# Hybrid block on one core: a ninth up tile in seven half products, adding transfers moved ahead, and a changed step into the MLP

## The chip, the cores and the metric

The kernel runs on 1 core of one Trainium2 chip. The metric is the device time in microseconds; the time before is 696.63 us, the median of 3 runs (695.25 to 696.77).

## The reference, cut to what matters

One layer of a trunk with x of 512 tokens by 1024 features. Attention of three kinds (A: differential, B: forgetting, C: chunked) is concatenated and goes through one out-projection; then comes a gated MLP of 2 x 2816 columns with a causal convolution of width 3; then a gated embedding of p.

```
h = h + jnp.concatenate([o_a, o_b, o_c], axis=-1) @ w_out[i]
h = h + conv_gated_mlp(rms_norm(h, ln_ffn[i]), w_up[i], conv_w[i], conv_b[i], w_down[i])
gate = jax.nn.sigmoid(rms_norm(h, ln_ple[i]) @ w_ple_gate[i])
h = h + (p[i] @ w_ple_proj[i]) * gate
...
u = h @ w_up
for j in range(CONV_WIDTH):
    c = c + conv_w[j] * up[:, j:j + S]
gate, val = jnp.split(c, 2, axis=-1)
return (jax.nn.silu(gate) * val) @ w_down
```

## The kernel before, in words

Matrix products run in three terms: each operand is split into a high part (a cast by ACT, names ending in hi, h or ah) and a low part (a subtraction by DVE, names ending in lo, l or al), and mm3 (line 238) issues high x high, low x high and high x low. So each weight tile costs a load into w_raw on SP's queue, an ACT cast w_hi, a DVE split w_lo, and then matmuls.

After the attention come the out-projection (last_out, tiles wo), the squares of its result for the norm (sq, sums, pst), and the projection of p (ple_unit, tiles pp, copied by ACT to pps and stored). roots takes the mean square in pst through a logarithm and an exponential on ACT into rb; norm(k) makes hn, Th (ACT) and Tl (DVE), the right sides of the MLP.

The MLP has 22 tiles of 128 gate and 128 value columns. An up tile is done in one of two forms:
- plain (up_plain, line 1254): two products u of 8 x 3 matmuls of 512 tokens, 48 in all, in three pieces of 18, 18 and 12;
- seven half products (up_seven, line 1278): 7 products of 12 matmuls of 256 columns, in banks sX, sZ, sZ2 and sY, in six pieces. Their left sides use sums of weight blocks that are added beforehand in memory (usum); the results are combined in su by ACT copies and DVE additions. The first two products go to sX and sZ; then Z2, Y, X again (after the first addition of su), Y again, and X a third time (after the second addition of su, which needs Y's second product).

ACT and DVE then make the taps of the convolution (c<-u or c<-su, a first one on ACT and two, of 511 and 510 columns, on DVE for each half), the silu on ACT and the multiplication c<-c,c on DVE. The down projection (dn_X, dn_Y, dn_Z) takes four groups of tiles in products of 18 matmuls of 256 columns, also with sums of weights (dsum); for the last groups the right sides are the tiles xh and xl.

What sets the order: the string ORDER (line 49) lists the pieces of the MLP on PE: P a piece of a plain tile, S a piece of a tile in seven half products, D one down product; tiles_of reads from it which tiles have which form. Before, the first two tiles stand outside of it, and tiles 4, 6, 9, 10, 12, 14, 16 and 18 have seven half products. The tasks of ACT, DVE and POOL around them are ordered by a planner from costs and dependences and then kept in the order written. PE, ACT, DVE and POOL each execute their rows in that order.

The sums of weights need two things. copy_sum (line 835) copies a part of a prepared sum from the inputs to a work tensor (usum of 256 KB or dsum), on SP's queue, at most two in each slot of the attention; COPIES spreads them over the slots 20 to 45 by the number of sums. add_sums makes one adding transfer after the other on POOL's queue, four for a usum and eight for a dsum, two in flight at a time; two_adds issues the first of these by hand, at fixed places of the program.

Of the kernel before, what the change touches and what calls it, by code (L numbers as in the profile page):

```python
# [45 lines left out]
PHASES = (0, 6, 12, 18, 22)  # L46


ORDER = ("PPPPSSSSSPPSPPSSSSPSPPSPPDDDDDDDSPSSSSDSDDDPDDDSSSSSPSPPSSSSSPSPSSSDSSDDDSDPDDDDDDDDDPPPSSSSSPPSPSSSPSSPSPPPPPPP")


def tiles_of(order):

    f, n, tiles = 2, {"P": 0, "S": 0}, {"P": [], "S": []}
    for c in order:
        if c in n:
            if n[c] == 0:
                tiles[c].append(f)
                f += 1
            n[c] = (n[c] + 1) % {"P": 3, "S": 6}[c]  # L60
    assert f == NF and not any(n.values()), (f, n)
    return tiles["P"], tiles["S"]


PLAIN, SEVEN = tiles_of(ORDER)

# [11 lines left out]
def kernel(ctx: ExitStack, tc: tile.TileContext, x, xt0, xt, pt_in, small, bias_c,  # L78
# [33 lines left out]
    pe, act, dve, pool, sp = (Engine(e) for e in (nc.tensor, nc.scalar, nc.vector, nc.gpsimd, nc.sync))  # L112

    def bank(tag, name):
        return ps.tile([P, 512], F32, tag=tag, bufs={"z": 2, "s": 2, "t": 3, "o": 1}[tag], name=name)
# [122 lines left out]
    def mm3(acc, ah, al, bh, bl, first, last, **k):  # L238
        pe.matmul(acc, ah, bh, start=first, stop=False, **k)
        pe.matmul(acc, ah, bl, start=False, stop=False, **k)  # L240
        pe.matmul(acc, al, bh, start=False, stop=last, **k)
# [598 lines left out]
    def add_parts(key):  # L840

        v, _, more = sums_of(key)
        pairs = ((1, more[:, 0]), (2, more[:, 1]), (0, v[:, 1]), (3, v[:, 0]))
        if key[0] == "u":
            return [(v[:, i], q) for i, q in pairs]
        return [(v[:, i, j], q[:, j]) for i, q in pairs for j in range(2)]
# [59 lines left out]
    def last_out(j):  # L906
        for _ in out_unit(j, (6, 7), {k: wo[k, j // 4] for k in (6, 7)}, []):
            pass
# [8 lines left out]
    def mtmp(dt, m, name):  # L917
        return mp.tile([P, S * m], dt, tag="conv", bufs=CONV, name=name)
# [3 lines left out]
    def square(j):  # L922
        sq = mtmp(F32, 1, f"sq{j}")
        act.activation(sq, hj(j), AF.Square)
        return sq

    def total(tag, sums):

        pst = bank(tag, "pst")
        pe.matmul(pst, onec.broadcast_to([P, P]), sums, start=True, stop=True)  # L930
        return pst

    def roots(pst, rb, mt, sq):

        act.activation(rb, pst, AF.Ln, scale=1.0 / D, bias=epsc)
        dve.tensor_scalar(mt, pst, 1.0 / D, EPS, ALU.mult, ALU.add)
        act.activation(rb, rb, AF.Exp, scale=-0.5)
        dve.tensor_tensor(out=sq, in0=rb, in1=rb, op=ALU.mult)
        dve.scalar_tensor_tensor(sq, sq, -0.5, mt, ALU.mult, ALU.mult)
        dve.scalar_tensor_tensor(rb, sq, 1.5, rb, ALU.add, ALU.mult)  # L940
# [20 lines left out]
    def ple_product(j):  # L961
        PP[j] = acc = bank("tttzsttt"[j], f"pp_{j}")
        for k in range(2):
            a, b = (w[:, j % 4 * P : (j % 4 + 1) * P] for w in WPP[j // 4, k])
            mm3(acc, a, b, *pT[k], k == 0, k == 1)

    def ple_keep(j):
        pp = mtmp(F32, 1, f"pps_{j}")
        act.copy(pp, PP[j])
        sp.dma_start(out=pp_d[j], in_=pp)  # L970

    def ple_unit(j):
        ple_product(j)
        ple_keep(j)
# [210 lines left out]
    def add_sums():  # L1185

        state = {}

        def do(to, src):
            ins = pool.dma_start(out=to, in_=src, accum_op=ALU.add, max_dma_last_dim=6144).ins  # L1190
            state["all"] = [*state.get("all", ()), ins]
            if len(state["all"]) > 2:
                tc.add_manual_dep(ins, state["all"][-3].name, mybir.DependencyInfo(
                    mybir.DependencyClass.Sync, mybir.DependencyReason.DATA), reason="two adding transfers at a time")

        adds = EARLY_ADDS
        for _, *key in _sums:
            key = tuple(key)
            for to, src in add_parts(key):
                adds.append(Task("add", [("pool", 0.85), (f"acc{len(adds) % 2}", 4.8 if key[0] == "u" else 5.2)], lambda to=to, src=src: do(to, src),  # L1200
                                 adds[-1:] if key[0] == "u" and len(SUM_TASKS.get(key, ())) == 3 else adds[-2:-1]))
                SUM_TASKS.setdefault(key, []).append(adds[-1])
# [200 lines left out]
    def first_load():  # L1403
        q = loads.pop(0)
        q.do()
        q.end = 0.0

    def first_split(f, i, later=False):
        w = first_w[f][0][i]
        lows = [] if later else None  # L1410
        w.hi, w.lo = split(w.t, w.n, lows=lows)
        w.split.end = 0.0
        return lows[0] if later else None

    def two_adds():
        for q in [q for q in EARLY_ADDS if q.end is None][:2]:
            q.do()
            q.end = 0.0

    add_sums()  # L1420
    act.pinned = dve.pinned = pool.pinned = True
    sums, todo = None, ple_splits()
    loads = first_loads()
    for _ in range(2):
        first_load()
    todo += [lambda i=i: first_split(0, i) for i in range(2)]
    for j in range(KD):
        last_out(j)
        if 0 < j < KD - 1:
            todo[j - 1]()  # L1430
            if j > 2:
                first_load()
        elif j:
            todo[6]()
        sq = square(j)
        if j == 1:
            sums = mtmp(F32, 1, "sums")
            pool.tensor_tensor(out=sums, in0=last_sq, in1=sq, op=ALU.add)
        elif j > 1:
            (pool if j < KD - 2 else dve).tensor_tensor(out=sums, in0=sums, in1=sq, op=ALU.add)  # L1440
        last_sq = sq
    todo[7]()
    two_adds()
    for j in range(3):
        ple_unit(j)
    first_split(1, 0)
    ple_unit(3)
    rb2, work = (mp.tile([P, 7, H], F32, tag=tag, bufs=3, name=f"rb2_{tag}").rearrange("p j c -> p (j c)") for tag in ("ah", "al"))
    rb2 = rb2[:, :S]
    roots(total("o", sums), rb2, work[:, :S], work[:, S : 2 * S])  # L1450
    ple_unit(4)
    last_low = first_split(1, 1, True)
    norm(0)
# [106 lines left out]
    pieces = {"P": (f for f in PLAIN for _ in up_plain(f)), "S": (f for f in SEVEN for _ in up_seven(f)), "D": down_pieces()}  # L1560
    for c in ORDER:
        next(pieces[c])
# [263 lines left out]
```

## Time and profile before

| what | value |
|---|---|
| median of 3 runs | 696.63 us |
| the profiled execution | 695.37 us, span 693.6 us |
| mean granted TensorE clock | 0.998 |
| PE, DVE, ACT, POOL busy | 679.1, 560.6, 410.9, 236.0 us |
| DMA | 133.84 MB, mean 193 GB/s |
| first and last product of the MLP | 309.47 and about 644 us |

A row of the timeline gives the start, the duration, the engine, the line of the program, the operation with out<-in, the shape and, in brackets, how long the engine was idle ahead of it and what released it. A line of the chain gives start, length, engine and tile. Line 104 is the helper that issues almost every operation, so rows are told apart by tiles.

### The profile page before, as it was taken

What the parts mean: (1) busy time and instruction counts of PE and PEld (TensorE: products, weight loads), DVE (VectorE), ACT (ScalarE), POOL (GpSimd) and SP (SyncE); (2) the same over time, 40 slices, a digit from 0 to 9 for tenths busy, and PEclk for the clock granted to TensorE, in tenths of its full rate; (3) what the DMA queues carried; (4) which work ended last, traced back from release to release, by engine and by line L of the source; (5) the groups of instructions that cost most, each with busy time, mean ns of one, the idle gap of its engine ahead of it and who ended that gap; (6) DMA issues with size and microseconds to landing.
All of it is one profiled execution on the core that took longest, in us unless ns stands there. A gap on an engine that the chain in (4) does not pass through costs nothing.

```text
span 693.6 us, 12203 instructions
## 1 busy us (share of the span) xinstructions
PE 679.1 (98%) x4244; PEld 618.3 (89%) x4244; DVE 560.6 (81%) x1168; ACT 410.9 (59%) x799; POOL 236.0 (34%) x349
## 2 busy tenths in 40 slices
PE   8999999999999999999999999999999999999997
PEld 8988988988999988878899899989998898999886
DVE  6679887888878875689788987898888889888873
ACT  6656766767656754475476655456554566556821
POOL 5586675767575540231212111221112200000210
PEclk9999999999999999999999999999999999999999
DMA  9553579746745184279999799997999874462431
GB/s 307 216 168 98 155 241 265 232 165 162 287 136 178 44 266 138 91 184 242 175 269 244 133 266 241 274 232 176 248 278 277 181 197 140 141 234 99 156 122 60
DMA packets 57112, 133.84 MB, mean 193 GB/s; under 512 B 6454, under 2 KB 8118, under 8 KB 57052
## 3 DMA queue, kind: packets, MB, share of 16 engines
q1 hardware_dynamic: 45660, 107.60, 47.0%
q0 software_dynamic: 11104, 25.17, 22.2%
q8 instruction: 33, 0.54, 0.3%
q10 hardware_dynamic: 288, 0.30, 0.1%
q14 instruction: 27, 0.22, 0.1%
HBM read 125.83 MB, written 44.05 MB: 245 GB/s over the span
## 4 chain that ended last, share of the span: by engine, by line
PE 83%; DVE 8%; ACT 3%; POOL 3%; issue 2%; DMA 1%; SPq 0%; DVEq 0%; POOLq 0%; ACTq 0%
PE u L104 22%; PE dn_X L104 9%; PE pg L104 6%; PE C_z L104 5%; PE wo L104 5%; PE sX L104 5%; PE dn_Y L104 4%; PE B_z L104 4%; PE sY L104 3%; PE sZ L104 3%; PE A_z L104 3%; PE dn_Z L104 2%; PE A1b_z L104 1%; PE C_s L104 1%; PE B_s L104 1%
## 5 line engine op out<-in xcount | busy, mean ns | idle before, releaser
L104 DVE TENSOR_TENSOR w_lo<-w_raw,w_hi 128x768 fp32r<-128x768 f32 (+5 forms) x154 | 115.0, 786 | 9.5 <-ACT w_hi L104 9.3
L104 ACT CAST w_hi<-w_raw 128x768 fp32r<-128x768 f32 (+5 forms) x154 | 99.8, 687 | 35.9 <-PE sX L104 6.7
L104 PE MATMUL u<-Th,w_hi 128*128 128x512 f32 x224 | 87.0, 391 | 0.4 <-ACT Th L104 0.4
L104 PE MATMUL u<-Tl,w_hi 128*128 128x512 f32 x224 | 86.9, 390 | 0.0
L104 PE MATMUL u<-Th,w_lo 128*128 128x512 f32 x224 | 86.8, 390 | 0.0
L104 PEld LDWEIGHTS u<-Th,w_hi 128*128 128x128 f32 x224 | 42.0, 188 | 9.1 <-ACT Th L104 0.9
L104 PEld LDWEIGHTS u<-Th,w_lo 128*128 128x128 f32 x224 | 42.0, 188 | 9.0
L104 PEld LDWEIGHTS u<-Tl,w_hi 128*128 128x128 f32 x224 | 42.1, 188 | 8.1
L104 DVE SCALAR_TENSOR_TENSOR c<-u,cols,c 128x511 f32<-128x511 f32 (+1 forms) x56 | 41.0, 746 | 6.2 <-ACT c L104 5.7
L104 POOL DMA_DIRECT2D usum<-usum x16 | 13.0, 812 | 92.5 <-DMA usum<-in_w_up_dram 56.7
L104 PE MATMUL dn_X<-g_ah,w_hi 128*128 128x256 f32 x144 | 39.8, 276 | 0.0
L104 PE MATMUL dn_X<-g_ah,w_lo 128*128 128x256 f32 x144 | 39.8, 276 | 0.0
L104 PE MATMUL dn_X<-g_al,w_hi 128*128 128x256 f32 x144 | 39.8, 276 | 0.0
L104 PE MATMUL B_z<-B_h,Th 128*128 128x384 f32 x96 | 34.4, 358 | 0.8 <-DVE B_zn L104 0.6
L104 PE MATMUL C_z<-C_h,Th 128*128 128x384 f32 x96 | 34.3, 357 | 0.0
L104 POOL TENSOR_TENSOR sums<-sums,n_sq 128x512 f32<-128x512 f32 x3 | 3.9, 1291 | 86.9 <-ACT n_sq L104 86.8
L104 PE MATMUL B_z<-B_h,Tl 128*128 128x384 f32 x96 | 32.3, 337 | 0.0
L104 PE MATMUL C_z<-C_h,Tl 128*128 128x384 f32 x96 | 32.3, 337 | 0.0
L104 PE MATMUL C_z<-C_l,Th 128*128 128x384 f32 x96 | 32.2, 336 | 0.0
L104 PE MATMUL B_z<-B_l,Th 128*128 128x384 f32 x96 | 32.2, 335 | 0.0
L104 ACT ACTIVATE c<-u,cols 128x512 f32<-128x512 f32 x28 | 21.5, 775 | 16.0 <-PE u L104 14.6
L104 POOL DMA_DIRECT2D dsum<-dsum x16 | 13.0, 813 | 47.2 <-DMA dsum<-dsum 20.0
(504 smaller groups left out, 2384.0 us busy)
## 6 DMA issues: line engine op xcount, KB each, us to landing
w_raw<-in_w_up_dram SPq DMA_DIRECT2D x44, 384.0 KB, 6.1
dsum<-in_w_dsum_dram SPq DMA_DIRECT2D x12, 768.0 KB, 7.9
w_raw<-dsum SPq DMA_DIRECT2D x24, 384.0 KB, 5.0
usum<-in_w_usum_dram SPq DMA_DIRECT2D x32, 256.0 KB, 6.1
w_raw<-in_w_down_dram SPq DMA_DIRECT2D x18, 384.0 KB, 4.9
w_raw<-usum SPq DMA_DIRECT2D x16, 384.0 KB, 7.7
B_r<-in_w_in_dram SPq DMA_DIRECT2D x12, 384.0 KB, 3.6
C_r<-in_w_in_dram SPq DMA_DIRECT2D x12, 384.0 KB, 6.1
```

The costliest lines, as they stand in the source:

```text
L104: ins = getattr(self.eng, op)(*a, **k)
```

## The change

Three things:
1. ORDER has another order of pieces, with 11 plain tiles and 9 in seven half products: tile 15 is now one of these. With it go four more copies and four more adding transfers.
2. Two adding transfers are issued during the out-projection, as soon as POOL's last operation ahead of it is done; the two calls of two_adds that were there stay. So six transfers are issued ahead of the MLP by hand, four before.
3. In the step into the MLP first_split(1, 0), the split of the second tile's first weights (w_hi6 and w_lo6), comes one ple unit earlier, and the copy pps of unit 3 comes behind roots (logarithm and exponential).

```
-ORDER = ("PPPPSSSSSPPSPPSSSSPSPPSPPDDDDDDDSPSSSSDSDDDPDDDSSSSSPSPPSSSSSPSPSSSDSSDDDSDPDDDDDDDDDPPPSSSSSPPSPSSSPSSPSPPPPPPP")
+ORDER = ("PPPPSPSSSSPSPPSSSSPSPSPPPDDDDPDPDDSSDSSDSDDSDDDSSSSSPPSPSSSSSPSPSSSDPDSSDSDDDDDDDDDDDSSSSSSSSSSSPSPPSSSSSPSPPPPPPPP")
...
     add_sums()
+    last_sum_free = pool.last
     act.pinned = dve.pinned = pool.pinned = True
...
     todo += [lambda i=i: first_split(0, i) for i in range(2)]
+    with tc.issue_after(last_sum_free):
+        two_adds()
     for j in range(KD):
         last_out(j)
...
     two_adds()
-    for j in range(3):
+    for j in range(2):
         ple_unit(j)
     first_split(1, 0)
-    ple_unit(3)
+    ple_unit(2)
+    ple_product(3)
...
     roots(total("o", sums), rb2, work[:, :S], work[:, S : 2 * S])
+    ple_keep(3)
     ple_unit(4)
```

ple_unit(j) is ple_product(j), the matmuls, followed by ple_keep(j), the copy and the store.

**PE at tile 15.** In the changed kernel the rows of PE where the sixth product of tile 15 (sY15) ends and the seventh (sX15) begins:

```order
L104 MATMUL sY15_6367<-Th1_65,w_lo2_3991 128x256
L104 MATMUL sY15_6367<-Th1_65,w_hi2_3990 128x256
L104 MATMUL sY15_6367<-Tl1_67,w_hi2_3990 128x256
L104 MATMUL sY15_6367<-Th1_65,w_lo2_3991 128x256
L104 MATMUL sX15_6316<-xh_3881,w_hi1_3974 128x256
L104 MATMUL sX15_6316<-xl_3882,w_hi1_3974 128x256
L104 MATMUL sX15_6316<-xh_3881,w_lo1_3975 128x256
L104 MATMUL sX15_6316<-xh_3881,w_hi1_3974 128x256
```

In the kernel before, PE's rows behind the sixth product of tile 16, which has the same form in both:

```order
L104 MATMUL sY16_6436<-Th1_65,w_lo5_4022 128x256
L104 MATMUL sY16_6436<-Th1_65,w_hi5_4021 128x256
L104 MATMUL sY16_6436<-Tl1_67,w_hi5_4021 128x256
L104 MATMUL sY16_6436<-Th1_65,w_lo5_4022 128x256
L104 MATMUL u17_6503<-Th0_64,w_hi6_4057 128x512
L104 MATMUL u17_6503<-Tl0_66,w_hi6_4057 128x512
L104 MATMUL u17_6503<-Th0_64,w_lo6_4058 128x512
```

There pieces of a plain tile stand between the sixth product and the seventh; at the new tile 15 nothing does.

**ACT in the step into the MLP.** Before, from the last square on (pps the copies, w_hi6 the split that moves, rb2_ah the logarithm and the exponential):

```order
L104 CAST w_hi5_4021<-w_raw5_3902 128x768
L104 COPY pps_0_4034<-pp_0_4027 128x512
L104 COPY pps_1_4044<-pp_1_4037 128x512
L104 COPY pps_2_4054<-pp_2_4047 128x512
L104 CAST w_hi6_4057<-w_raw6_3953 128x768
L104 COPY pps_3_4068<-pp_3_4061 128x512
L104 ACTIVATE rb2_ah_4071<-pst_4073,epsc_76 128x512
L104 ACTIVATE rb2_ah_4071<-rb2_ah_4071 128x512
L104 COPY pps_4_4088<-pp_4_4081 128x512
```

The same rows in the changed kernel:

```order
L104 CAST w_hi5_4029<-w_raw5_3908 128x768
L104 COPY pps_0_4042<-pp_0_4035 128x512
L104 COPY pps_1_4052<-pp_1_4045 128x512
L104 CAST w_hi6_4055<-w_raw6_3961 128x768
L104 COPY pps_2_4066<-pp_2_4059 128x512
L104 ACTIVATE rb2_ah_4076<-pst_4078,epsc_76 128x512
L104 ACTIVATE rb2_ah_4076<-rb2_ah_4076 128x512
L104 COPY pps_3_4086<-pp_3_4069 128x512
L104 COPY pps_4_4096<-pp_4_4089 128x512
```

One copy has moved behind the two ACTIVATE rows, and the cast of w_hi6 ahead of one copy.

**DVE ahead of the last down products.** Before, from the first taps of tile 20 to those of tile 21 (c20 and c21 the gate halves, c42 and c43 the value halves):

```order
L104 SCALAR_TENSOR_TENSOR c20_7004<-u20_6820,cols_84,c20_7004 128x511
L104 SCALAR_TENSOR_TENSOR c42_7006<-u42_6839,cols_84,c42_7006 128x511
L104 SCALAR_TENSOR_TENSOR c20_7004<-u20_6820,cols_84,c20_7004 128x510
L104 SCALAR_TENSOR_TENSOR c42_7006<-u42_6839,cols_84,c42_7006 128x510
L104 TENSOR_TENSOR w_lo5_4022<-w_raw5_3902,w_hi5_4021 128x768
L104 TENSOR_TENSOR xl_3877<-sm_18_7001,xh_3876 128x1024
L104 TENSOR_TENSOR c20_7004<-c20_7004,c42_7006 128x512
L104 SCALAR_TENSOR_TENSOR c21_7061<-u21_6883,cols_84,c21_7061 128x511
L104 SCALAR_TENSOR_TENSOR c43_7064<-u43_6909,cols_84,c43_7064 128x511
L104 SCALAR_TENSOR_TENSOR c21_7061<-u21_6883,cols_84,c21_7061 128x510
L104 SCALAR_TENSOR_TENSOR c43_7064<-u43_6909,cols_84,c43_7064 128x510
L104 TENSOR_TENSOR c21_7061<-c21_7061,c43_7064 128x512
```

The same place in the changed kernel:

```order
L104 SCALAR_TENSOR_TENSOR c20_7065<-u20_6858,cols_84,c20_7065 128x511
L104 SCALAR_TENSOR_TENSOR c42_7067<-u42_6877,cols_84,c42_7067 128x511
L104 SCALAR_TENSOR_TENSOR c20_7065<-u20_6858,cols_84,c20_7065 128x510
L104 SCALAR_TENSOR_TENSOR c21_7095<-u21_6932,cols_84,c21_7095 128x511
L104 SCALAR_TENSOR_TENSOR c21_7095<-u21_6932,cols_84,c21_7095 128x510
L104 SCALAR_TENSOR_TENSOR c43_7099<-u43_6955,cols_84,c43_7099 128x511
L104 SCALAR_TENSOR_TENSOR c42_7067<-u42_6877,cols_84,c42_7067 128x510
L104 SCALAR_TENSOR_TENSOR c43_7099<-u43_6955,cols_84,c43_7099 128x510
L104 TENSOR_TENSOR w_lo0_3958<-w_raw0_3898,w_hi0_3957 128x768
L104 TENSOR_TENSOR xl_3882<-sm_18_7062,xh_3881 128x1024
L104 TENSOR_TENSOR c20_7065<-c20_7065,c42_7067 128x512
L104 TENSOR_TENSOR c21_7095<-c21_7095,c43_7099 128x512
```

The second tap of c42, a split of 768, the split of xl and the multiplication of c20 stood ahead of tile 21's taps and now stand behind the first of them. From there on to the split of dn3_0_1e, the first weights of the last group, the rows are the same in both kernels.

More of the change, by code (lines that the diff above doesn't have):

```diff
@@ L46 @@
 PHASES = (0, 6, 12, 18, 22)
-ORDER = ("PPPPSSSSSPPSPPSSSSPSPPSPPDDDDDDDSPSSSSDSDDDPDDDSSSSSPSPPSSSSSPSPSSSDSSDDDSDPDDDDDDDDDPPPSSSSSPPSPSSSPSSPSPPPPPPP")
+ORDER = ("PPPPSPSSSSPSPPSSSSPSPSPPPDDDDPDPDDSSDSSDSDDSDDDSSSSSPPSPSSSSSPSPSSSDPDSSDSDDDDDDDDDDDSSSSSSSSSSSPSPPSSSSSPSPPPPPPPP")
 def tiles_of(order):
@@ L1420 @@
     add_sums()
+    last_sum_free = pool.last
     act.pinned = dve.pinned = pool.pinned = True
@@ L1426 @@
     todo += [lambda i=i: first_split(0, i) for i in range(2)]
+    with tc.issue_after(last_sum_free):
+        two_adds()
     for j in range(KD):
@@ L1443 @@
     two_adds()
-    for j in range(3):
+    for j in range(2):
         ple_unit(j)
     first_split(1, 0)
-    ple_unit(3)
+    ple_unit(2)
+    ple_product(3)
     rb2, work = (mp.tile([P, 7, H], F32, tag=tag, bufs=3, name=f"rb2_{tag}").rearrange("p j c -> p (j c)") for tag in ("ah", "al"))
@@ L1450 @@
     roots(total("o", sums), rb2, work[:, :S], work[:, S : 2 * S])
+    ple_keep(3)
     ple_unit(4)
```

## The prediction

> **What bounds the kernel now.** I read the busy shares first, then the chain that ended last, then the windows of the MLP.
>
> ```profile
> PE 679.1 (98%) x4244; PEld 618.3 (89%) x4244; DVE 560.6 (81%) x1168; ACT 410.9 (59%) x799; POOL 236.0 (34%) x349
> PE 83%; DVE 8%; ACT 3%; POOL 3%; issue 2%; DMA 1%; SPq 0%; DVEq 0%; POOLq 0%; ACTq 0%
> 500.00:550.00 50.00, 50.00 (x347) 46.17 (x345) 44.08 (x71) 27.41 (x45) 10.60 (x13) 1.00 1.01 255
> 595.00:644.00 49.00, 49.00 (x427) 48.72 (x426) 41.64 (x62) 30.13 (x48) 1.81 (x2) 1.00 0.47 163
> ```
>
> PE is busy for 98% of the span and carries 83% of the chain. In the two windows of the MLP (after the stretch: its length, then PE, PEld, DVE, ACT, POOL busy, the granted clock, the DMA share) PE is busy for all of 50.00 and 49.00 us at a clock of 1.00. So in the MLP one microsecond of matmul less is one less of time, and one microsecond in which PE has to wait is one more. DVE is next: 44.08 of 50.00 us. It has little room to catch up, and it executes in the order written, so a row moved ahead of another delays what stands behind.
>
> **Tile 15 as seven half products.** The chain of the last MLP stretch has tile 15 in its plain form in one piece and tile 16 in the other form in several.
>
> ```profile
> 522.86 10.91 PE u L104 x48
> 533.77 1.39 PE sX L104 x12
> 535.17 2.72 PE sZ L104 x24
> 537.89 1.36 PE sY L104 x12
> 539.25 1.36 PE sX L104 x12
> 540.61 1.36 PE sY L104 x12
> 541.97 8.19 PE u L104 x36
> 550.16 1.40 PE sX L104 x12
> ```
>
> The plain tile: 48 matmuls, 10.91 us. The other: 84 matmuls, 1.39 + 2.72 + 1.36 + 1.36 + 1.36 + 1.40 = 9.59 us. The change turns one tile from the first into the second: **-1.3 us**, all of it on PE. The new order of the other units adds and removes no matmul.
>
> **A wait that this tile brings.** The last row above is the seventh product (sX for the third time). It adds to the bank that the second adding of su reads, and that adding needs the sixth product (sY for the second time). In tile 16 there are 8.19 us of other products between the two. In the changed order of tile 15 there is nothing between them. How long the chain from the sixth to the seventh takes is seen at tile 10 (the single matmul is the last of sY, then ACT's copy, then DVE's addition):
>
> ```profile
> 451.53 0.28 PE L104 MATMUL sY<-Th,w_lo 128*128 128x256 f32 x1
> 451.65 0.40 PE L104 MATMUL u<-Th,w_hi 128*128 128x512 f32 x1
> 451.85 0.37 ACT L104 COPY su<-sY 128x256 f32<-128x256 f32 x1 [1.10 <-PE sY L104]
> 452.25 0.42 DVE L104 TENSOR_TENSOR su<-sX,su 128x256 f32<-128x256 f32 x1 [0.43 <-ACT su L104]
> ```
>
> PE issued the next matmul at 451.65. The addition ended at 452.67; with some 0.07 us to release PE, the seventh product could have begun at 452.74. So the wait is 452.74 - 451.65 = **+1.1 us**. Bounds: 0 if the planner's order is not what is executed (nothing speaks for it), and about 1.9 if one more cast as long as the longest shown below (0.85) stands in the way. In the changed order ACT's row ahead of the copy is a cast of 512 and DVE's is an old multiplication of sm; DVE waits there itself, so I take 1.1. Behind DVE's waiting row stand two splits of g and splits of w_lo, all for products that stand later in PE's order and move back with it, so I cost them at nothing; if one of them is needed first, the upper bound has it.
>
> **The changed step into the MLP.** Here the path is not PE: it goes from the sum of squares over ACT and DVE to Th.
>
> ```profile
> 301.06 0.82 ACT L104 CAST w_hi<-w_raw 128x768 fp32r<-128x768 f32 x1
> 301.78 1.55 ACT L104 COPY pps<-pp 128x512 f32<-128x512 f32 x3
> 303.21 0.85 ACT L104 CAST w_hi<-w_raw 128x768 fp32r<-128x768 f32 x1
> 303.94 0.61 ACT L104 COPY pps<-pp 128x512 f32<-128x512 f32 x1
> 304.42 0.72 ACT L104 ACTIVATE rb_ah<-pst,epsc 128x512 f32<-128x512 f32 x1
> 308.64 0.39 PE L104 MATMUL pp<-pT_ah,w_lo 128*128 128x512 f32 x1
> 308.80 0.62 ACT L104 CAST Th<-hn 128x512 fp32r<-128x512 f32 x1 [1.79 <-DVE hn L104]
> 309.47 0.50 PE L104 MATMUL u<-Th,w_hi 128*128 128x512 f32 x1 [0.44 <-ACT Th L104]
> ```
>
> The logarithm of rb_ah began at 304.42, when the copy of pps ahead of it was done; the copy held ACT from 303.94 to 304.42. The change puts that copy behind the logarithm and the exponential: the logarithm, and with it everything to Th and u, comes 0.48 us earlier, **-0.48 us**. PE's idle time there is 309.47 - 308.64 - 0.23 (the issue of one matmul of 512, 308.64 less the one ahead) = 0.60 us, so 0.48 fits into it. What is late next is PE itself, 0.12 us behind. The copy that moved frees a bank that no product before u needs. Bounds: 0 to -0.60.
>
> **DVE's order at the last down products.** In the new order the taps of tile 21 stand ahead of a split of 768, the split xl of sm_18 (1024) and the multiplication of c20. DVE's rows there now (c is a tap or multiplication, xl a right side, and the last DVE row the split that PE's product at 606.74 needs):
>
> ```profile
> 591.66 0.95 DVE L104 TENSOR_TENSOR w_lo<-w_raw,w_hi 128x768 fp32r<-128x768 f32 x1
> 592.52 1.22 DVE L104 TENSOR_TENSOR xl<-sm,xh 128x1024 fp32r<-128x1024 f32 x1
> 593.66 0.69 DVE L104 TENSOR_TENSOR c<-c,c 128x512 f32<-128x512 f32 x1
> 596.15 0.75 DVE L104 SCALAR_TENSOR_TENSOR c<-u,cols,c 128x511 f32<-128x511 f32 x1 [1.81 <-ACT c L104]
> 597.52 2.06 DVE L104 SCALAR_TENSOR_TENSOR c<-u,cols,c 128x511 f32<-128x511 f32 x3 [0.61 <-ACT c L104]
> 599.69 0.69 DVE L104 TENSOR_TENSOR c<-c,c 128x512 f32<-128x512 f32 x1
> 600.30 0.42 DVE L104 TENSOR_TENSOR sm<-c 128x256 f32<-128x256 f32 x1
> 605.92 0.68 DVE L104 TENSOR_TENSOR w_lo<-dn_1e,w_hi 128x512 fp32r<-128x512 f32 x1
> 606.97 0.28 PE L104 MATMUL dn_X<-xh,w_lo 128*128 128x256 f32 x1
> ```
>
> The tap at 596.15 waits for the last product of its u, so it cannot come earlier; DVE idled 1.81 us ahead of it because all it could do was done. In the new order four rows that ran before that idle time stand behind it. One second tap falls into the idle 0.61 us at 597.52, since tile 21's own second tap moves there. Three remain: 592.52 - 591.66 = 0.86, 593.66 - 592.52 = 1.14 and 600.30 - 599.69 = 0.61, in all 2.6 us. About 0.1 of it fits into the gap between 599.58 and 599.69, where a multiplication waits for ACT. So the split that ended at 606.60 ends 2.5 us later. PE read it at 606.97, 0.37 after its end, of which some 0.09 is the release: 0.28 us of room. The wait is 2.5 - 0.28 = **+2.2 us**. The splits behind it are late too, but PE needs each at least 1.3 us after the one before, so the wait is paid once. PE has no idle time up to 644 (row above), so it reaches the end. Bounds: 1.6 by adding DVE's rows back to back from the tap on, without the small gaps that it shows between rows; 2.6 with no room at all.
>
> **Adding transfers and copies.** From the view of the tile usum (when the second transfers of a sum are issued, and ACT's only wait, once, for what lies in usum), and from the out-projection's timeline and DMA issues:
>
> ```profile
> L104 POOL DMA_DIRECT2D usum<-usum x16: 807/812/821, 306.8 to 488.4; - x16
>   ACT w_hi L104: 1.4, 1
> 267.00 0.62 ACT L104 CAST wo_h<-wo_r 128x512 fp32r<-128x512 f32 x1 [1.67 <-DMA wo_r<-in_w_out_dram]
> 271.09 0.62 ACT L104 CAST wo_h<-wo_r 128x512 fp32r<-128x512 f32 x1 [1.79 <-DMA wo_r<-in_w_out_dram]
> dsum<-in_w_dsum_dram SPq DMA_DIRECT2D x1, 512.0 KB, 5.7
> 277.56 0.63 PE L104 MATMUL C_po<-ptc,C_V 128*128 128x256 f32 x4
> 278.24 0.58 ACT L104 COPY C_ot<-C_po 64x512 f32<-64x512 f32 x1 [5.76 <-PE C_po L104]
> ```
>
> Between 306.8 and 488.4 all sums of the up tiles are added, one pair behind the other; at 488.4 the last is under way, and tile 16, which isn't the last of its kind, begins at 533.77 (above). One pair more ahead of the MLP and four transfers more on the whole leave each sum in place at about the time at which it is now. Cost **0**, hidden by this lead of tens of us; a wait of the size of ACT's 1.4 us is the upper bound, none below 0. POOL issues the early pair when its last attention row is done; behind it stands a split of wo that now starts 21 us after that row, so nothing there waits. The four more copies run on SP's queue in the attention, and one (512 KB) now stands ahead of the load of wo that ACT took at 271.09. That ACT row has room: behind it come 0.53 on ACT, 0.61 and 0.55 on DVE, and PE reads the result at 277.56, so it may begin as late as about 275.8. Cost 0; bounds 0 to +2 (below).
>
> The Trainium skill, page "DMA: Bandwidth & Descriptors", section "Issuing engines are not separate DMA queues", says that transfers started by different engines run on the same 16 DMA engines and interleave, which speaks against adding POOL's transfers to a stretch where ACT waits for SP's. The trace agrees so far as the waits of 1.67 and 1.79 us show loads that are late already; by that rule the sum would be that of the third rival.
>
> **The sum**, against the profiled execution's 695.37 us (span 693.6 and 1.8 around it): -1.3 - 0.48 + 1.1 + 2.2 + 0 = +1.5, 696.9. That execution lies 1.26 us below the median of the runs shown, 696.63; I add the 1.5 to the median: **698.1 us**.
>
> **Rivals.**
> 1. *Only one of the two waits is there.* For it: DVE's rows vary by some tenths, and a wait upstream (at tile 15) gives DVE time that a later split then has. Against: the tail's count starts from a tap that is tied to PE's own progress, so an earlier wait gives nothing back. Without the tail's wait 698.1 - 2.2 = 695.9, without the other 697.0. Chance 0.2.
> 2. *Not slower: neither wait reaches PE.* PE has other work queued only in its order, so this needs the executed order to differ from the one listed, or PE to be held at those places by something of before. Then the shorter tile and the earlier logarithm are all: 696.63 - 1.8 = 694.8. It decides at the point where DVE's late split still ends before PE's read, that is if less than 0.3 us of the 2.6 lands behind the tap. Chance 0.1.
> 3. *The load of wo comes late.* The extra copy of 512 KB and the two early transfers stand ahead of it or beside it. The copy of this size that stands there now took 5.7 us to land (row above). If the added one delays the load by as much, ACT's row moves to 271.09 + 5.7 = 276.8, and PE loses 276.8 - 275.8 = 1.0; I put up to 2 with the adding transfers beside it. 698.1 + 1.0 = 699.1. Against: several copies are in flight at once, so the delay should be a part of the 5.7. Chance 0.2.
>
> **How the numbers follow.** The forecast has 0.5 and its own range is 697.3 to 699.0: the tail's 1.6 in place of 2.2 and 0.2 less elsewhere at the low end, tile 15's wait at its upper bound at the high end. The measurement can tell about 0.2%, 1.39 us, so slower begins at 698.0: just under half of the forecast's range lies below it, 0.23, with rival 1's 0.2 that makes 0.42 for the same. Slower: 0.27 and rival 3's 0.2, 0.48 rounded up. Faster: rival 2's 0.1. Leaving out that rival and the upper half of the third, the range is 695.7 to 699.6.
>
> **What would show it.** Right: tile 15's pieces of PE together take 9.6 us plus one gap of about 1.1 us between sY and the sX behind it, released by DVE su; the logarithm at about 303.9 and u's first matmul released 0.48 us earlier; DVE idle nearly 3 us, not 1.81, ahead of the tap of tile 21, and PE idle some 2 us at the first dn_X product that reads xh, released by DVE w_lo. Wrong: a PE that has no idle time at one of these two places; PE waiting for C_po or wo near 277; PE waits in the middle of the MLP, where two splits of w_lo (near 438 and 486 in the changed order) have by my count of DVE's rows only 0 to 0.5 us of room; or loads of w_raw for tile 15's larger weights that come late.

## The result and the profile after

The changed kernel takes **701.38 us** (median of 7 runs, 698.3 to 705.3) against 696.63 us (7 runs): ratio **1.0067, 95% interval 1.0044 to 1.0089**. A second set of runs of it gave 700.98 us, 1.0066 (1.0046 to 1.0086). So it is slower by 4.6 to 4.75 us; 1.5 was forecast, and the range ended at 699.6. The profiled execution took 703.04 us, its span is 701.3 us, the mean granted clock 0.997.

First, the page of the changed kernel: the busy shares and the shares of the chain.

```profile
PE 681.5 (97%) x4280; PEld 620.9 (89%) x4280; DVE 564.5 (80%) x1172; ACT 412.3 (59%) x804; POOL 240.4 (34%) x354
PE 78%; DVE 8%; DMA 4%; POOL 4%; issue 3%; ACT 3%; SPq 0%; POOLq 0%; DVEq 0%; ACTq 0%
```

PE's share of the chain fell from 83 to 78%, that of DMA rose from 1 to 4%. So a part of the loss is waiting for transfers, and I split the time at the first product of the MLP. It begins at 314.12 us (309.47 before) and the span ends at 701.3 (693.6): behind that point 387.15 us against 384.13, **+3.0 us**, and ahead of it **+4.65 us** in this execution. The first number repeats in a second trace of the changed kernel; the second doesn't (312.5 us there), of which more below.

The windows of the MLP at about the places of the two shown of before; the order differs, so the work in them is not quite the same (after the stretch: its length, then PE, PEld, DVE, ACT, POOL busy, clock, DMA share):

```profile
504.00:554.00 50.00, 49.08 (x405) 47.91 (x404) 43.30 (x65) 28.77 (x47) 9.78 (x12) 1.00 1.02 259
598.50:651.70 53.20, 51.45 (x437) 50.47 (x435) 45.31 (x67) 32.26 (x51) 1.95 (x2) 1.00 0.47 158
```

PE, which was busy for all of both windows, now lacks 0.92 and 1.75 us. The two forecast waits lie in these windows.

**Tile 15.** PE's rows at the end of its sixth product (sY) and the start of the seventh (sX), then ACT's and DVE's rows of su:

```profile
535.93 0.28 PE L104 MATMUL sY<-Th,w_lo 128*128 128x256 f32 x1
537.13 0.39 PE L104 MATMUL sX<-xh,w_hi 128*128 128x256 f32 x1 [0.92 <-DVE su L104]
537.35 0.28 PE L104 MATMUL sX<-xl,w_hi 128*128 128x256 f32 x1
536.24 0.37 ACT L104 COPY su<-sY 128x256 f32<-128x256 f32 x1 [1.20 <-PE sY L104]
536.65 0.42 DVE L104 TENSOR_TENSOR su<-sX,su 128x256 f32<-128x256 f32 x1 [0.79 <-ACT su L104]
```

A matmul of 256 issues 0.11 us after the one ahead. So PE waits 537.13 - 535.93 - 0.11 = 1.09 us for the addition that ended at 537.07, and the matmul behind the first is late by another 0.11.

**The last down products.** DVE from the last taps of tile 20 on:

```profile
596.95 2.06 DVE L104 SCALAR_TENSOR_TENSOR c<-u,cols,c 128x511 f32<-128x511 f32 x3
601.40 3.50 DVE L104 SCALAR_TENSOR_TENSOR c<-u,cols,c 128x511 f32<-128x511 f32 x5 [2.40 <-ACT c L104]
604.82 0.95 DVE L104 TENSOR_TENSOR w_lo<-w_raw,w_hi 128x768 fp32r<-128x768 f32 x1
605.69 1.22 DVE L104 TENSOR_TENSOR xl<-sm,xh 128x1024 fp32r<-128x1024 f32 x1
606.83 1.29 DVE L104 TENSOR_TENSOR c<-c,c 128x512 f32<-128x512 f32 x2
613.66 0.68 DVE L104 TENSOR_TENSOR w_lo<-dn_1e,w_hi 128x512 fp32r<-128x512 f32 x1
```

DVE idles 2.40 us (1.81 before) ahead of tile 21's first tap, and what it did ahead of that tap before runs behind it now. PE, where the first products reading xh follow:

```profile
611.88 0.28 PE L104 MATMUL dn_Y<-g_ah,w_lo 128*128 128x256 f32 x1
612.93 0.38 PE L104 MATMUL dn_X<-xh,w_hi 128*128 128x256 f32 x1 [0.78 <-ACT w_hi L104]
613.15 0.28 PE L104 MATMUL dn_X<-xl,w_hi 128*128 128x256 f32 x1
614.40 0.39 PE L104 MATMUL dn_X<-xh,w_lo 128*128 128x256 f32 x1 [0.96 <-DVE w_lo L104]
614.62 0.28 PE L104 MATMUL dn_X<-xh,w_hi 128*128 128x256 f32 x1
```

It waits 0.94 us for ACT's cast and 1.14 for DVE's split, and the matmul behind each of these is late by another 0.11: 2.30 us.

**The step into the MLP.** PE at the first product of u:

```profile
313.76 0.39 PE L104 MATMUL pp<-pT_ah,w_lo 128*128 128x512 f32 x1
314.12 0.73 PE L104 MATMUL u<-Th,w_hi 128*128 128x512 f32 x2
```

The idle time ahead of it is 314.12 - 313.76 - 0.23 = 0.13 us; it was 0.60.

**The out-projection.** ACT's cast of the tile of wo that was taken at 267.00 before, behind a wait of 1.67 us:

```profile
276.47 0.62 ACT L104 CAST wo_h<-wo_r 128x512 fp32r<-128x512 f32 x1 [6.87 <-DMA wo_r<-in_w_out_dram]
```

It waits 6.87 us for its load. What ACT does next is late, and PE waits for DVE's ptc, which needs a cast of ACT:

```profile
281.84 0.28 PE L104 MATMUL C_po<-ptc,C_V 128*128 128x256 f32 x1
282.39 0.62 PE L104 MATMUL C_po<-ptc,C_V 128*128 128x256 f32 x3 [0.28 <-DVE ptc L104]
282.99 0.50 PE L104 MATMUL wo<-Th,wo_h 128*128 128x512 f32 x1
```

### The profile page after: what moved, and what is told of

The parts are those of the page before. It is cut to its first block, busy times and chain, and to the rows that moved or that the text cites. A ratio compares the mean times of both kernels' runs of the same rounds, so it can differ in the third digit from the quotient of the medians.

```text
span 701.3 us, 12311 instructions
## 1 busy us (share of the span) xinstructions
PE 681.5 (97%) x4280; PEld 620.9 (89%) x4280; DVE 564.5 (80%) x1172; ACT 412.3 (59%) x804; POOL 240.4 (34%) x354
## 4 chain that ended last, share of the span: by engine, by line
PE 78%; DVE 8%; DMA 4%; POOL 4%; issue 3%; ACT 3%; SPq 0%; POOLq 0%; DVEq 0%; ACTq 0%
PE u L104 20%; PE dn_X L104 8%; PE pg L104 6%; PE C_z L104 5%; PE sX L104 5%; PE B_z L104 4%; PE wo L104 4%; PE dn_Y L104 4%; PE sY L104 4%; PE sZ L104 4%; PE A_z L104 3%; PE dn_Z L104 2%; PE pp L104 2%; DMA wo_r<-in_w_out_dram 1%; PE C_s L104 1%
## 5 line engine op out<-in xcount | busy, mean ns | idle before, releaser
L104 DVE TENSOR_TENSOR w_lo<-w_raw,w_hi 128x768 fp32r<-128x768 f32 (+5 forms) x155 | 117.5, 792 | 10.0 <-ACT w_hi L104 9.2
L104 PE MATMUL u<-Th,w_hi 128*128 128x512 f32 x208 | 80.8, 391 | 0.0
L104 PE MATMUL u<-Tl,w_hi 128*128 128x512 f32 x208 | 80.7, 390 | 0.0
L104 PE MATMUL u<-Th,w_lo 128*128 128x512 f32 x208 | 80.6, 390 | 0.0
L104 PEld LDWEIGHTS u<-Th,w_lo 128*128 128x128 f32 x208 | 39.1, 188 | 8.3
L104 PEld LDWEIGHTS u<-Th,w_hi 128*128 128x128 f32 x208 | 39.0, 188 | 8.0 <-ACT Th L104 0.4
L104 PEld LDWEIGHTS u<-Tl,w_hi 128*128 128x128 f32 x208 | 39.1, 188 | 7.5
L104 DVE SCALAR_TENSOR_TENSOR c<-u,cols,c 128x511 f32<-128x511 f32 (+1 forms) x52 | 37.9, 745 | 8.7 <-ACT c L104 8.2
L104 POOL DMA_DIRECT2D usum<-usum x18 | 14.6, 812 | 78.4 <-DMA usum<-in_w_up_dram 33.1
L104 ACT ACTIVATE c<-u,cols 128x512 f32<-128x512 f32 x26 | 19.7, 775 | 21.2 <-PE u L104 20.4
```

The source lines that it names most:

```text
L104: ins = getattr(self.eng, op)(*a, **k)
```

## The experiments

Each ratio is to the kernel before, run on the same chip in the same job; 0.1% is 0.7 us. The last column is the start of the MLP's first product in the trace.

| kernel | median us | ratio (95%) | MLP from |
|---|---|---|---|
| after_again | 700.98 | 1.0066 (1.0046-1.0086) | 312.5 |
| before_again | 696.42 | 0.9994 (0.9976-1.0011) | 310.0 |
| step_only | 695.70 | 0.9989 (0.9976-1.0002) | 310.3 |
| early_only | 698.36 | 1.0024 (1.0010-1.0037) | 311.4 |
| copies_only | 698.07 | 1.0022 (1.0010-1.0035) | 310.8 |
| copies_again | 696.97 | 1.0013 (1.0001-1.0025) | 313.6 |
| copies_more | 696.97 | 1.0003 (0.9985-1.0021) | 310.6 |
| slots_only | 696.32 | 0.9997 (0.9988-1.0005) | 311.3 |
| step_early | 697.42 | 1.0018 (1.0002-1.0034) | 311.6 |
| step_copies | 696.62 | 1.0003 (0.9988-1.0019) | 310.6 |
| front_only | 699.40 | 1.0051 (1.0037-1.0064) | 311.2 |
| after_no_early | 699.79 | 1.0059 (1.0038-1.0080) | 310.6 |
| after_copies_moved | 701.23 | 1.0068 (1.0050-1.0087) | 310.9 |
| after_tail | 705.40 | 1.0104 (1.0070-1.0138) | 314.8 |
| after_tail2 | 699.70 | 1.0028 (1.0011-1.0045) | 314.0 |
| tail2_no_early | 698.37 | 1.0024 (1.0013-1.0035) | 312.6 |
| after_split15_tail | 703.66 | 1.0106 (1.0086-1.0127) | 311.7 |
| best0 | 700.71 | 1.0049 (1.0029-1.0068) | 311.1 |

### How far one trace can be trusted

> The changed kernel once more, for a second trace. Theory 1 (the four copies that fill the four slots with a single copy delay loads of the attention): 701.4 us, and the same PE waits near 145, 189 and 277 us as in the first trace, 1.1, 0.9 and 0.6 us more than before. Theory 2 (the attention differs from execution to execution, and the 7 runs happened to be late): the waits lie elsewhere and the time is between 697 and 700 us.

> The kernel before, unchanged, as a second trace of it and as a measure of how far two sets of runs of one kernel differ. Ratio within 0.9990 to 1.0010. If the small waits ahead of the MLP that stand in the traces of the changed kernel and not in the first trace of the kernel before (PE behind the loads of bias_B and bias_C and at 40 to 60 us) are chance, some of them stand in this trace too and the first product of the MLP begins later than 309.5; if they are the change's, it begins at 309.3 to 309.7.

The times came as expected, 700.98 us by the first theory of after_again and 0.9994. The places did not: near 189 us, where the first trace of the changed kernel falls 1.1 us further behind the kernel before, the second loses nothing. Behind the first product of the MLP, after and after_again agree (387.15 and 387.14 us), and the two traces of before likewise (384.13 and 384.11); ahead of it they differ by 1.6 and by 0.57 us. The clearest case is a pair of identical kernels below, copies_only and copies_again. The first product of u in each:

```profile
310.76 1.20 PE L105 MATMUL u<-Th,w_hi 128*128 128x512 f32 x4 [0.45 <-ACT Th L105]
```

```profile
313.61 0.74 PE L105 MATMUL u<-Th,w_hi 128*128 128x512 f32 x2 [0.45 <-ACT Th L105]
```

One program, 2.85 us apart. More than half of this is the clock. The same stretch of both, copies_only first (columns as above; the granted clock stands ahead of the DMA share):

```profile
46.40:49.60 3.20, 3.20 (x21) 3.20 (x20) 2.53 (x5) 0.98 (x3) 2.57 (x6) 1.00 0.32 68
46.40:49.60 3.20, 3.20 (x13) 3.15 (x12) 2.39 (x4) 1.16 (x3) 2.43 (x5) 0.50 0.37 103
```

In copies_again the granted clock is 0.50 here, and PE issues 13 matmuls, not 21. Matched matmul by matmul, it lies 0.3 us behind copies_only at 42 us, loses 0.8 in a wait that ends at 46.0 and 1.6 at half the clock. The first copy of a sum into a work tensor is issued at 67.92 us in copies_only and at 70.84 in copies_again, so the whole difference is there by then. Eight of the twenty traces have such a stretch of 3.4 us between 44 and 50 us (after, after_tail, after_tail2, after_split15_tail, tail2_no_early, copies_again, step_only, step_early). In these the first copy is issued at 69.2 to 70.8 us, in the other twelve at 67.5 to 68.9: 1.4 us on the mean.

So ahead of the MLP a single trace tells where a wait is, but not what a change costs; the medians do, to about 1 us.

### The parts ahead of the MLP, each alone in the kernel before

step_only has the third part of the change, as in the diff above.

> The kernel before with only the changed step into the MLP. By the prediction 0.48 us faster than before, 696.1 us, the logarithm earlier by 0.48 and PE's idle time ahead of u 0.1 in place of 0.6 us. Rival: the copies that now follow the exponential hold a bank or ACT, and nothing is gained: 696.6 us.

It gave 0.9989: -0.8 us (-1.7 to +0.1). In its trace u begins 11.91 us after the first product of pp, not 12.39: 0.48 less, as in all traces of kernels with this step (11.90 to 11.92).

early_only has the early pair:

```
     add_sums()
+    last_sum_free = pool.last
...
+    with tc.issue_after(last_sum_free):
+        two_adds()
     for j in range(KD):
```

> The kernel before with only the early pair of adding transfers. Theory 1 (the pair, on the same DMA engines, delays the loads of wo that ACT waits for near 267 and 271): 0.3 to 0.9 us slower than before, 696.8 to 697.4 us, with a PE wait at C_po near 277. Theory 2 (the loads have room): no change, 696.5 us within 0.4, no such wait.

It gave 1.0024, **+1.7 us** (0.7 to 2.6), more than the first theory's 0.3 to 0.9. copies_only adds four copies, into a spare tensor, in the slots of the changed kernel; copies_again is the same kernel; copies_more has sixteen (`for _f in (5, 8, 11, 15)`); slots_only gives the 48 old copies the slots that they have in copies_only, without the four:

```
+_copied = sorted([*_sums, (15, "x", 15)])
-for _i, _q in enumerate(_sums):
+for _i, _q in enumerate(_copied):
...
+                if key[0] == "x":
+                    SUMS[key] = dp.tile([P, 4, 512], F32, tag="spare", name="spare"), w_usum[f], None
```

> The kernel before with only the four more copies, in the slots that the changed kernel uses (they copy the sums of tile 4 a second time into a spare tensor that nothing reads). Theory 1: 2.0 to 3.5 us slower than before, 698.6 to 700.1 us, with the same waits near 145, 189 and 277 us. Theory 2: no change, 696.6 us within 0.7.

> The kernel with four more copies once more. Theory (those four cost something where they stand): +1.0 to +2.0, 697.5 to 698.5. Rival (the first measurement was at the edge of chance, as sixteen copies at +0.2 suggest): -0.5 to +0.7.

> The kernel before with 16 more copies of 256 KB (the prepared sum of tile 4 four times into four spare tensors), spread over the same slots. Theory A (copies compete with the loads of the attention, in proportion): four cost 1.5, so 16 cost 4 to 8 us, 700.5 to 704.5. Theory B (what costs is a single collision with one load, or where tensors lie in memory): 697.5 to 699. Theory C (the 1.5 us of four copies was chance): 696.2 to 697.2.

> The 48 copies of the kernel before in the slots that they have when four more stand among them, without these four. If moving the others into other slots is what costs: as much as copies_again. If the added copies cost: 696.2 to 697.0. If neither costs, all of these agree within 0.1%.

Four copies measured +1.5 and +0.9 us, between the two theories of both runs, sixteen +0.2 (-1.0 to +1.5), the other slots -0.2. A cost in proportion is out: it would have made 4 to 6 us of sixteen. Four may cost some 1 to 1.5 us, but these runs don't show it as a property of the copies.

### The parts together, with the old order of the MLP

front_only has all three parts, step_early leaves out the copies, step_copies the early pair.

> The kernel before with all that the change does ahead of the MLP and nothing of what it does in it: four more copies (of tile 4's sum, into a spare tensor), the early pair of adding transfers and the changed step; the order of the MLP is the old one. Theory (the two halves of the change add up, and what is lost ahead of the MLP comes from these parts): 4.6 - 3.05 = +1.5, 697.7 to 698.7, ratio 1.002 to 1.003; ACT waits 6 to 7 us for wo_r in the out-projection and PE 0.5 to 1.4 us behind it, or, in an execution where that load comes in time, neither. Rival (what is lost ahead of the MLP comes with the whole program, not with these parts): 696.0 to 696.8.

> The kernel before with the changed step and the early pair, without the four copies. Theory (the early pair is the larger cost: the loads of wo, and of the weights of tile 5, land late behind it): -0.5 + 1.7 = +1.2, ratio 1.0015 to 1.003; ACT waits 6 to 7 us for wo_r in the trace. Rival (the copies carry it): -0.5 to +0.3, ratio under 1.0005.

> The kernel before with the changed step and the four copies, without the early pair. Theory (the early pair is the larger cost): -0.5 + 0.8 = +0.3, ratio 0.9995 to 1.001. Rival (the copies carry it): +1.5 to +2.5, ratio 1.002 to 1.0035.

front_only at 1.0051, in five runs, lies above the 1.002 to 1.003 expected: with the old order of the MLP, the parts ahead of it make the kernel **slower by 2.6 to 4.5 us**, though the step in it gains. Against step_only (0.9989) the early pair adds 0.29%, 2.0 us, and the copies 0.14%, 1.0 us, each with some 1.4 us of uncertainty either way.

The traces say how the pair costs. step_early, ACT's wait for wo in the out-projection:

```profile
274.02 0.62 ACT L104 CAST wo_h<-wo_r 128x512 fp32r<-128x512 f32 x1 [6.88 <-DMA wo_r<-in_w_out_dram]
```

copies_more, with sixteen copies more and no early pair:

```profile
268.32 0.62 ACT L105 CAST wo_h<-wo_r 128x512 fp32r<-128x512 f32 x1 [1.82 <-DMA wo_r<-in_w_out_dram]
```

All nine traces of kernels with the early pair have this wait at 6.7 to 7.1 us, all eleven without it at 1.6 to 2.6 us, with and without the added copies. PE pays for it in five of the nine: its way from the first product of the out-projection to the start of the last group of them is longer by 0.8 to 1.4 us than in the kernel before, by 0.06 us or less in the other four and in all eleven without the pair; 0.6 us on the mean of the nine. What decides whether PE pays, these runs don't show.

The pair has a second price in the old order of the MLP only. step_early, ACT behind the loads of the weights of tile 5, and PE where u of tile 5 begins:

```profile
360.67 0.93 ACT L104 CAST w_hi<-w_raw 128x128 fp32r<-128x128 f32 x2 [1.94 <-DMA w_raw<-in_w_up_dram]
364.78 0.28 PE L104 MATMUL sX<-xh,w_lo 128*128 128x256 f32 x1
367.13 0.47 PE L104 MATMUL u<-Th,w_hi 128*128 128x512 f32 x1 [2.07 <-DVE c L104]
```

PE waits 2.24 us there, 0.8 in early_only, 0.2 in front_only, and in no trace of the changed kernel, whose order has other pieces at that place. In early_only the two prices are 0.8 us each, together 1.6 of the 1.7 measured.

### The early pair and the copies within the changed kernel

after_no_early is the changed kernel without the two lines of the early pair; after_copies_moved puts tile 15's copies as a third one into slots 38 to 41 and leaves the others as before.

> The changed kernel without the early pair: the same adding transfers, one pair later. Theory 1: the PE wait at C_po shrinks from 0.6 to 1.0 us to 0.3 or less, and the time falls by 0.3 to 0.9, 700.3 us; nothing in the MLP waits for a sum. Theory 2 (the early pair is needed for the sums): new PE waits in the MLP released by ACT w_hi or a transfer, 701.5 us or more.

> The changed kernel with the 48 other copies in the slots of the kernel before and tile 15's four as a third copy in the slots 38 to 41. Theory 1: 1.5 to 3 us faster than the changed kernel, 698.4 to 699.9 us, and near 145 and 189 us PE waits as long as before. Theory 2: 701.4 us as the changed kernel.

Without the pair ACT's wait is back at its old size:

```profile
268.55 0.62 ACT L104 CAST wo_h<-wo_r 128x512 fp32r<-128x512 f32 x1 [1.61 <-DMA wo_r<-in_w_out_dram]
```

The time fell by 0.07% only (0.5 us, with some 2 us of uncertainty either way). Moving the copies changed nothing (1.0068). What the 16 DMA engines did meanwhile, over five microseconds from the issue of the first of these loads of wo, in the changed kernel (the pair was issued 2 us earlier) and in after_no_early over the same piece of work (last columns: DMA share, GB/s):

```profile
268.60:273.60 5.00, 5.00 (x29) 4.23 (x28) 2.51 (x5) 0.94 (x2) 0.00 (x0) 1.00 0.83 94
```

```profile
265.95:270.95 5.00, 5.00 (x29) 4.23 (x28) 3.85 (x7) 2.72 (x5) 0.00 (x0) 1.00 0.68 197
```

With the pair the engines are busy for 83% of the time and move 94 GB/s; without, 68% and 197. The first load of wo, the one that ACT waits for, is issued at the same point of the work and takes 7.8 us to land, in place of 2.5 in after_no_early; the four loads of wo issued there take 8.6 us (the median), in place of 6.2, though both kernels have the second 512 KB copy among them. The Trainium skill, page "DMA: Bandwidth & Descriptors", section "Issuing engines are not separate DMA queues", says that transfers share the 16 engines whichever engine started them; these rows agree, and show in addition that with the adding transfers under way the engines are busier and move half as much.

### The order at tile 21

after_tail makes DVE's taps of tile 21 wait for the rows that stood ahead of them before; after_tail2 does the same for ACT's first copy of tile 21:

```
+    for q in (NAMED["start", 21], NAMED["tap", 21, 0, 1], NAMED["tap", 21, 1, 1]):
+        q.after += [NAMED["tap", 20, 1, 2], NAMED["split", "dn2_1_1e"], NAMED["four", 18], NAMED["end", 20]]
```

(after_tail has the two taps alone; NAMED is a table of the planner's tasks.)

> The changed kernel with the taps of tile 21 planned behind the split of dn2_1_1e, the split xl of sm_18 and the multiplication of c20, as before. By the prediction's step: the two PE waits at the last down products (0.9 for ACT w_hi and 1.1 for DVE w_lo) go, 2.3 us with the slower matmuls behind them, 698.8 us. Rival: DVE is short of time there in any order, since a tile in seven half products costs it more, and 1 us or more of the wait stays: 699.8 us or above.

> The changed kernel, with both engines held to the old order at tile 21: ACT's casts of two weight tiles and DVE's splits, the split xl of sm_18 and the multiplication of c20 all stand ahead of ACT's first copy and DVE's first tap of tile 21. Theory (the 2.29 us at the first dn2 products that read xh come from DVE rows that run behind tile 21's taps for no need, and nothing else holds that place): both waits of PE go or fall under 0.5 us in all, and the time is 701.0 - 2.3 = 698.7 (698.2 to 699.2). Rival (something else, loads or ACT, is late there as well): PE still waits over 1 us at that place and the time stays at 700 to 701.

after_tail did not mend it: DVE's split moved ahead, but its cast stayed behind ACT's copy of tile 21, so DVE stood and waited:

```profile
603.01 0.96 DVE L104 TENSOR_TENSOR w_lo<-w_raw,w_hi 128x768 fp32r<-128x768 f32 x1 [2.72 <-ACT w_hi L104]
```

PE's waits there even grew, to 1.30 and 1.13 us, and the clock fell behind them (last section). Of its six runs the two with a mean granted clock of 0.998 took 699.28 and 701.36 us, the four with 0.991 to 0.995 took 705.40 to 706.29. With ACT's order mended too, in after_tail2, DVE has the rows done in time:

```profile
600.65 1.82 DVE L104 TENSOR_TENSOR w_lo<-w_raw,w_hi 128x768 fp32r<-128x768 f32 x2
602.38 2.71 DVE L104 SCALAR_TENSOR_TENSOR c<-u,cols,c 128x511 f32<-128x511 f32 x4
611.42 0.68 DVE L104 TENSOR_TENSOR w_lo<-dn_1e,w_hi 128x512 fp32r<-128x512 f32 x1
```

and PE goes on without a gap:

```profile
612.09 0.28 PE L104 MATMUL dn_Y<-g_ah,w_lo 128*128 128x256 f32 x1
612.20 0.28 PE L104 MATMUL dn_X<-xh,w_hi 128*128 128x256 f32 x1
612.32 0.28 PE L104 MATMUL dn_X<-xl,w_hi 128*128 128x256 f32 x1
612.43 0.28 PE L104 MATMUL dn_X<-xh,w_lo 128*128 128x256 f32 x1
```

The ratio falls from 1.0066 (1.0046 to 1.0086) to 1.0028 (1.0011 to 1.0045), by 0.38% or 2.6 us (with some 1.8 us of uncertainty). In the traces the time behind the first product of the MLP falls from 387.15 to 385.15 us: 2.30 us of waits are gone, and the one at tile 15 is 0.32 longer. So the order of DVE and ACT is the cause of these waits. DVE's order alone doesn't mend it (after_tail); ACT's alone was not run.

> The changed kernel with the old order of ACT and DVE at tile 21 and without the early pair. Theory (the early pair costs what the late wo_r loads show, 0.7 on the mean of seven traces, and nothing else): 0.7 below the kernel with the early pair (ratio 1.0028), so 1.0018, 697.9. Upper case (its 0.24% when alone): 1.0004, 696.9. Rival (it costs nothing beside the other parts): 1.0028, 698.6. Either way not below the kernel before.

At 1.0024 it is the fastest of the changed kernels and still slower than the kernel before; the pair is worth 0.3 us there, with some 1.4 us of uncertainty.

### Tile 15's wait

after_split15_tail (after_tail and one piece of a plain tile ahead of the sixth piece of tile 15) and best0 (after_tail2 without the early pair, a plain piece behind the fifth piece and another behind the sixth) take the plain pieces from behind tile 16:

```
-DSSSSSSSSSSSPSPP   changed kernel
+DSSSSSPSSSSSSPSP   after_split15_tail
+DSSSSSPSPSSSSSPS   best0
```

> The same, and a piece of the plain tile 17 moved between the sixth and the seventh product of tile 15 (the pieces of tiles 15 to 17 in the order SSSSS P SSSSSS P S P). By the prediction's step a further 1.2 us go, 697.6 us, and no PE wait of over 0.3 us is left behind the first u. Rival: the wait of DVE for su was hiding work that is now late elsewhere, and the gain is under 0.6: 698.3 us or above.

> The same order at tile 21, without the early pair of adding transfers, and with one piece of a plain tile behind the fifth and one behind the sixth piece of tile 15, so that neither its sixth nor its seventh product waits. Theory (the costs add up): 701.0 - 2.3 for the tail - 1.2 for tile 15's wait - 1.2 to 1.7 for the early pair = 695.8 to 696.3, as fast as the kernel before but not faster, since the shorter tile's 1.4 is used up by its four copies. Rival (each wait that is removed comes back elsewhere, as in the run that did both by halves): 698 to 700, with new waits of PE over 0.4 us behind tile 15. Rival (copies cost nothing): 694.5 to 695.

Tile 15's wait went in both, and others came. after_split15_tail took 703.66 us, above the 697.6 of its theory and within its rival's 698.3 or more: PE waits 0.95 us at 540.05 and 0.99 at 609.62, and the clock falls as in after_tail. In best0 the plain pieces are missing at tile 18:

```profile
555.77 0.36 PE L104 MATMUL sX<-Th,w_hi 128*128 128x256 f32 x1 [0.58 <-ACT g_ah L104]
563.68 0.39 PE L104 MATMUL sX<-xh,w_hi 128*128 128x256 f32 x1 [2.21 <-DVE su L104]
```

These are 0.7 and 2.4 us for the 1.2 saved. The rival expected for it (waits come back elsewhere) is right in the two orders that were tried; that nine tiles in seven half products leave too few plain pieces in any order is not shown.

## Why the prediction was wrong

*Right, by its own steps.* Tile 15 as seven half products: 48 matmuls of 512 fewer and 84 of 256 more are -48 x 0.227 + 84 x 0.1134 = -1.37 us (forecast -1.3). Its wait: 1.09 us, for the row forecast, DVE su (+1.1). The step into the MLP: -0.48 us, to the hundredth, with 0.13 us of idle time left (0.12 said). The last down products: 2.30 us (+2.2), by the rows and at the place that were named; only that PE waits twice, for ACT's cast and then for DVE's split, where one wait was forecast, and that DVE idles 2.40 us, not nearly 3. after_tail2 shows this cause by taking it away.

*The step that failed* is "Adding transfers and copies", put at 0 and "hidden by this lead of tens of us". The argument looked at when the sums are needed, and at POOL's next row. It did not ask what the two transfers do to the loads that run at the same time. They make wo land late in every trace that has them: ACT waits 6.9 us in place of 1.7. I had computed that ACT's second cast may begin at 275.8 and no later, and seen that SP's loads were late already; the third rival drew that conclusion, but gave its 1.0 us to the copy of 512 KB and the adding transfers only what lies above. The runs show the other bearer: with the copy and without the pair, ACT waits 1.61 us; with the pair and without the copy, 6.88. PE's loss in the changed kernel is 0.9 us in the first trace and 1.4 in the second, of the size of that rival's 1.0 to 2; on the mean of the traces with the pair 0.6.

*Terms that were missed in size.* The wait of PE costs 0.11 us more than its length, three times: 0.33. Waits that were put at nothing: 0.10 + 0.12 at a product of tile 4 and 0.16 + 0.11 near 492, one of the two places named (the other has none), 0.49 together:

```profile
361.86 0.28 PE L104 MATMUL sX<-xh,w_lo 128*128 128x256 f32 x1
362.07 0.39 PE L104 MATMUL sY<-Th,w_hi 128*128 128x256 f32 x1
492.30 0.28 PE L104 MATMUL dn_X<-g_al,w_hi 128*128 128x256 f32 x1
492.57 0.39 PE L104 MATMUL dn_X<-g_ah,w_lo 128*128 128x256 f32 x1
```

*The account.* Behind the first product of the MLP: -1.37 + 1.20 + 2.30 + 0.49 = +2.62 of the 3.0 measured (forecast +2.0); 0.4 us are not assigned, and no other wait of 0.1 us stands between the products of the MLP. The 3.0 with the step, -0.48, and the early pair, +0.6, make +3.1 of 4.6 us. Some 1.5 us remain (0.1 to 2.9 by the interval of the ratio), ahead of the out-projection, where the change has the copies alone.

The traces mix two things there. One is the stretch at half the clock near 45 us, which the first trace of the changed kernel has and the second hasn't; two kernels without added copies have it too, so the copies don't make it. The other is the time from the issue of the first copy to the first product of the out-projection: 172.3 to 174.3 us in the six traces without added copies (mean 173.2), 173.9 to 176.8 in the thirteen with four (174.5), 173.4 in the one with sixteen. That is 1.3 us more with four copies, as the medians' 0.9 to 1.5 say; but sixteen cost 0.2, and other slots nothing. **What these 1.5 us are stays open**; that they are the copies is argued, not shown.

*The rivals.* The first two (one wait or none) are refuted by the rows; the third happened, by the adding transfers. The range left out the upper half of that rival, had no room for the small waits, and so ended 1.8 us too low.

## What to carry to other kernels

A transfer that is hidden by its own deadline may still delay those of others: ask which loads run beside it and which of them an engine already waits for. Where two engines work in turn (a cast, then a split), an order forced on one of them only moves the wait. And where time ahead of a stage varies by microseconds from execution to execution, split a trace at that stage: the side that repeats to 0.1 us can be read from one trace, the other side from medians alone. Look at the granted clock by windows first: the mean over the span (0.998 in both traces of the copies kernel) hid a stretch at 0.50.

None of the changed kernels beats the kernel before. The changed step alone is the only part with a gain in its median, -0.11% (interval -0.24 to +0.02), within what the measurement can tell.

## What was not expected of the hardware

- After a wait of PE the first matmul of 256 columns is followed 0.22 us later (537.13 to 537.35), then 0.11 to 0.12 again; 0.19 to 0.23 at the waits of the MLP in these traces. So some 0.1 us comes on top of a wait, even of one of 0.10 us (362.07).
- Waits close together went with a lower granted clock. In after_tail PE lacked 2.08 of 4 us at these products, and the clock was 0.50 for 3.4 us behind (615.8 to 619.2); in after_split15_tail 2.07 of 4 us, and 0.50 from 614.6 to 617.9; in the changed kernel, with 1.75 lacking, it stayed at 1.00. But the share that PE lacks doesn't decide alone: ahead of the stretch near 45 us after_split15_tail lacked 1.64 of 3.40 us and got 0.50, best0 lacked 2.06 of 3.40 at that place and kept 1.00. after_tail's windows (columns as above):

```profile
612.00:616.00 4.00, 1.92 (x13) 1.52 (x13) 3.82 (x7) 3.64 (x8) 0.00 (x0) 0.97 0.94 324
616.00:618.00 2.00, 2.00 (x12) 2.00 (x10) 1.38 (x3) 2.00 (x4) 0.00 (x0) 0.50 1.04 361
618.00:620.00 2.00, 2.00 (x14) 2.00 (x14) 2.00 (x4) 1.01 (x2) 0.00 (x0) 0.70 1.05 399
```

  From 616 to 620 us 26 matmuls were issued where the changed kernel issues 40: 14 x 0.113 = 1.6 us. From the matmul that stands 36 ahead of the first one reading xh to the end of the MLP's products after_tail needs 45.8 us, the changed kernel 43.8, after_tail2 and the kernel before 41.5.
- With two adding transfers under way the DMA engines were 83% busy at 94 GB/s, without them 68% busy at 197 GB/s over the same work (rows above), and a load of 256 KB landed in 7.8 us, not 2.5.
